# A hybrid decoder layer on one core: table strips shifted on chip, and the order of the odd output projections

## The chip, the cores and the metric

The kernel runs on 1 core of one Trainium2 chip. The metric is device time in microseconds (us) of one execution; several executions are given by their median.

## What is computed

One decoder layer on x (2048 positions x 1024 channels), all in float32, cut to what matters:

```python
hn = rmsnorm(x, norm_g)
a_in, a_gate, c_in, c_b, c_c, c_gate, q, q_gate = split(hn @ w_in)   # 384 x6, 256 x2
# A: 24 groups of 16 channels, each a diagonal complex state space of 64 states
s[l] = lam_bar * s[l-1] + b_bar @ u[l];  y = Re(C s) + D u
g = gelu(y);  y_ssm = g * sigmoid(g @ w_glu + b_glu) * silu(a_gate)
# B: short causal convolution of width 3
y_conv = c_b * conv3(c_c * c_in) * silu(c_gate)
# M: 4-head attention from the positions into 256 fixed memory tokens
y_mem = softmax(q k^T / 8) v * silu(q_gate)
out = rmsnorm(x + concat(y_ssm, y_conv, y_mem) @ w_out, final_norm_g)
```

## The kernel before

**Tiling.** The 2048 positions are four quarters of 512 columns. Every float32 operand of a large matmul is split into a high and a low part (`split`, L86: a cast on ScalarE, L87, and a subtraction on VectorE, L78), and each product is three matmuls (`mm3`, L80, lines 82 to 84). Weights come in tiles of 512 KB through `wtile` (L159): a load on SP into one of two staging buffers, then the split into one of three buffers. An output row tile of a projection is 512 columns of one accumulation bank.

**Stages.** `first` prepares quarter 0; `prep(q)` (L731) loads the input rows of a quarter in four tiles of 128, sums their squares on ScalarE (L112), scales them and transposes them into the quarter's normalised input `hn`, which has one buffer. For each quarter the main line is a chain of projections (`ain`, `agate`, `qproj`, `qgate`, `conv`). `ssm(hf)` (L527) handles two quarters at once in eight tables of three groups: states per chunk of eight positions, a scan on VectorE, then outputs; its results go to DRAM (`g_dram`, L604) and come back in another layout in `glu(q)` (L998, `gr`), which splits them, multiplies by `w_glu`, gates, and splits the three gated state tiles (L1016). That last split overwrites what all nine products of the quarter's gate read. `attention(q, j)` (L917) has nine steps for each of two pairs of heads. `outproj(q)` (L1067) adds the residual and normalises. Quarters 1 and 3 are projected straight from on-chip results; 0 and 2 park theirs in DRAM.

**Tables.** `gen_table(b)` (L427) runs four times, for six groups each. It makes the products M and R, then the short kernel of each group (`ps_k`, L459; `kS`, L460) and its value at distance 0 (`k0r`, L465 and L466), transposes them (L469) and assembles `Kp`, 96 rows of 15 x 16 numbers (L470). `Kp` goes to `k_dram` (L471), and eight transfers (L474), one per position of a chunk, read it back, each shifted by 16 columns, into the table's fourth section, all on GpSimd's queue. One copy (L476) reorders that section, and the table is stored in `t_dram` (L479). Tables use two buffers of the pool `stab`, tag `tb`. `gen_turns` (L482) makes the rotation factors in buffers of the pool `xst`, tag `x`, which the input rows of `prep(1)` use next, and stores them in `t_dram` (L494).

**Order.** Each part is a generator, and the nesting of `interleave`, `weave`, `merge` and `chain` (L820 to L856) fixes the order in which instructions are traced: so many steps of a side line per step of the main line, by a rate. A scheduler then fixes each engine's queue when the program is built: with a clock of its own estimates it takes, for each engine, the earliest traced instruction whose inputs and buffers it holds to be ready. On the chip each queue runs in that order and waits where an estimate was short. The lines that set the order around the change are these (L1189 to L1204):

```python
a0 = att(0)
interleave(chain(kv, ain1), islice(a0, 6), 1.5)
interleave(chain(agate(1), qproj(1), conv(1, 0), qgate(1), conv(1, 1), conv(1, 2)),
           chain(merge(ssm(0), chain(a0, att(1)), 0.6), glu(1)), 3.7)
...
interleave(outproj(1), prep(2), 0.3, 2)
...
interleave(chain(ain(3), main(3)), chain(merge(ssm(1), att(3), 0.3), glu(3)), 3.5, 4)
fetch_y(2)
interleave(outproj(3), glu(2), 1.0)
```

**Output projection.** For each half of the 1024 columns, `outproj` takes the eight 128-row pieces of y in four steps of two: step 0 is state tiles 0 and 1, step 1 state tile 2 and convolution tile 0, step 2 convolution tiles 1 and 2, step 3 attention. Even quarters take them as 0, 1, 3, 2 (`pairs`), odd ones as 3, 2, 1, 0 (`back`, L1021). The residual rows are loaded at its start, on GpSimd's queue (L1060), into the two buffers `big0` and `big1` that attention's probabilities use.

Of the kernel before, what the change touches and what calls it, by code (L numbers as in the profile page):

```python
# [46 lines left out]
def hymba_layer_kernel(  # L47
# [96 lines left out]
    g_dram = dram.tile([NQ, WS, QL], F32, name="g_dram")  # L144
    k_dram = dram.tile([NB, GB * NH, 15 * NH], F32, name="k_dram")
    t_dram = dram.tile([NS, P, GS * TR], F32, name="t_dram")
# [42 lines left out]
    def st_(name, shape=(P, NG)):  # L189
        return sconst.tile(list(shape), F32, name="s_" + name)  # L190
# [8 lines left out]
    Eh, Gm = st_("Eh", (GB * NH, NH)), st_("Gm", (GB * NH, GB))  # L199
    Kp = st_("Kp", (GB * NH, 15 * NH))  # L200
    kS = st_("kS", (P, GB * NH))
    k0S, k0r = st_("k0S", (GB * NH, GB, NH)), st_("k0r", (GB * NH, NH))

    def ssm_prologue():
# [218 lines left out]
        V.tensor_reduce(Eh, idq.rearrange("q g h -> q h g"), AX.X, ALU.add)  # L423
        G.memset(Kp[:, 0:7 * NH], 0.0)


    def gen_table(b):  # L427
# [34 lines left out]
        flat = lambda a: a[:, gs, :].rearrange("p g h -> p (g h)")  # L462
        T.matmul(k0.rearrange("q g h -> q (g h)"), flat(B1), flat(R0), start=True, stop=True)
        tt(k0S, k0, Gm.unsqueeze(2).broadcast_to([GB * NH, GB, NH]), ALU.mult)
        V.tensor_reduce(k0r, k0S.rearrange("q g h -> q h g"), AX.X, ALU.add)  # L465
        V.scalar_tensor_tensor(Kp[:, 7 * NH:8 * NH], Eh, Dc[:, b:b + 1], k0r, ALU.mult, ALU.add)  # L466
        yield
        kb = ps_tr.tile([P, P], F32, tag="tr", name=f"tr_k{b}")[:GB * NH]
        T.transpose(kb, kS, ident)  # L469
        S.copy(Kp[:, 8 * NH:].rearrange("q (t h) -> q h t", h=NH), kb.rearrange("q (h t) -> q h t", h=NH)[:, :, :TCH - 1])  # L470
        nc.gpsimd.dma_start(k_dram[b], Kp)  # L471
        Tq = sec[:, :, 3]
        for j in range(TCH):
            nc.gpsimd.dma_start(Tq[j::TCH], k_dram[b].rearrange("(g h) n -> h g n", h=NH)[:, :, (TCH - 1 - j) * NH:(TCH - 1 - j) * NH + P])  # L474
        yield
# [150 lines left out]
    def first():  # L626
# [6 lines left out]
        wa = [wsl.tile([P, 2, KT, P], F32R, tag="wl", name=f"wai{t}") for t in range(3)]  # L633
        ngt, ones = pro.tile([1, DM], F32, name="ngt"), pro.tile([1, P], F32, name="ones")
        wm = pro.tile([P, QL], mybir.dt.bfloat16, name="wm")
        junk = stab.tile([P, DM], F32, tag="tb", name="junkx")
        ks = ((0, 2), (2, 4), (4, 8))
# [204 lines left out]
    def merge(a, b, rate):  # L842
# [9 lines left out]
        yield from b  # L852

    def chain(*gens):
        for g_ in gens:
            yield from g_  # L856
# [128 lines left out]
    def glu(q):  # L985
# [10 lines left out]
        for t in range(3):  # L996
            gr = swk.tile([P, QL], F32, tag="ain", bufs=2, name=f"gr{q}{t}")
            nc.gpsimd.dma_start(gr, g_dram[q, t * P:(t + 1) * P])  # L998
            split(y_ssm[:, 0, t], y_ssm[:, 1, t], gr)
            yield  # L1000
# [19 lines left out]
    yk = [("ssm", 0), ("ssm", 1), ("ssm", 2), ("conv", 0), ("conv", 1), ("conv", 2), ("mem", 0), ("mem", 1)]  # L1020
    pairs, back = (0, 1, 3, 2), (3, 2, 1, 0)  # L1021

# [26 lines left out]
    def residual(q, last=False):  # L1049

        if last:
            h = [late["att"].tile([P, DM], F32, tag="qh", bufs=2, name=f"h{q}{i}") for i in range(2)]
            for i in range(2):
                load_x(h[i], q, i)
            hb = late["big"].tile([P, 2, DM], F32, tag="big0", name=f"h{q}")
            return h + [hb[:, i] for i in range(2)], hb
        h = [late["big"].tile([P, 2, DM], F32, tag=f"big{z}", name=f"h{q}{z}") for z in range(2)]
        for z in range(2):
            for u in range(2):
                nc.gpsimd.dma_start(h[z][u * NCH:(u + 1) * NCH], xq[q, u][:, 2 * z:2 * z + 2])  # L1060
        return h

    def wout(q, nh, kp, dst=None, st="w"):
        src = w_out[0, kp * 256:(kp + 1) * 256, nh * 512:(nh + 1) * 512]
        return wtile(src, 256, 512, f"wo{q}{nh}{kp}", V, dst, st)

    def outproj(q):  # L1067
        h = residual(q)
        for nh in range(2):
# [4 lines left out]
            for kp in order:  # L1074
                w = wout(q, nh, kp)
                for i in range(4):
                    omm(q, pss[i], i, kp, w, ps_=order)
                    yield
# [107 lines left out]
    def att(q):  # L1186
        return chain(attention(q, 0), attention(q, 1))

    a0 = att(0)  # L1189
    interleave(chain(kv, ain1), islice(a0, 6), 1.5)  # L1190
    interleave(chain(agate(1), qproj(1), conv(1, 0), qgate(1), conv(1, 1), conv(1, 2)),
               chain(merge(ssm(0), chain(a0, att(1)), 0.6), glu(1)), 3.7)

    def main(q):
        return chain(qproj(q), agate(q), qgate(q), conv(q, 0), conv(q, 1), conv(q, 2))

    interleave(outproj(1), prep(2), 0.3, 2)
    interleave(chain(ain(2), main(2)), merge(glu(0), att(2), 0.5), 1.5, 4)
    fetch_y(0)
    interleave(outproj(0), prep(3), 0.3, 2)  # L1200
    interleave(chain(ain(3), main(3)), chain(merge(ssm(1), att(3), 0.3), glu(3)), 3.5, 4)
    fetch_y(2)
# [31 lines left out]
```

## Time and profile before

| what | value |
|---|---|
| runs | 893.05, 894.93, 895.01 us; median 894.93 |
| the profiled execution | 894.48 us, of which its span 892.7 us |
| TensorE (PE) busy | 838.2 us, 94% of the span |
| VectorE (DVE) busy | 612.6 us, 69% |
| ScalarE (ACT) busy | 393.9 us, 44% |
| GpSimd (POOL) busy | 52.4 us, 6% |
| transfers issued by SP and ScalarE | 130.6 MB, 50.1% of 16 engines' span |
| transfers issued by GpSimd | 11.38 MB, 5.2% |
| mean granted TensorE clock | 0.967 |

The span runs from the first to the last instruction of one execution that the hardware profiler took. Busy time is a sum over the whole span; where an engine idles shows only in the views by stretch and by wait. A matmul's shown duration overlaps that of the next, so rates are read from the count in a stretch. A wait names the engine and line that ended it last. The granted clock is TensorE's, as a share of full speed. SP and the queue parts of other engines (SPq, ACTq) count as no busy time.

### The profile page before, as it was taken

How to read it: one execution, taken by the hardware profiler on the slowest of the kernel's cores; microseconds unless marked ns; L12 is line 12 of the kernel's file. 1: busy time of each engine (PE TensorE's matmuls, PEld its weight loads, DVE VectorE, ACT ScalarE, POOL GpSimd, SP SyncE). 2: the span in 40 equal slices, each digit the busy share in tenths (PEclk: the TensorE clock that was granted, in tenths of full speed). 3: DMA queues.
4: the chain of work that ended last, by engine and by line, in shares of the span. 5: the costliest groups of instructions: out<-in, count | busy, mean ns of one | idle time of the engine just before them, and what ended most of it. 6: DMA issues, size and time to landing. Idle time of an engine off the chain costs nothing. (4 is left out here: it accounts for less than half of the span.)

```text
span 892.7 us, 11743 instructions
## 1 busy us (share of the span) xinstructions
PE 838.2 (94%) x4182; PEld 693.4 (78%) x4182; DVE 612.6 (69%) x1287; ACT 393.9 (44%) x767; POOL 52.4 (6%) x93
## 2 busy tenths in 40 slices
PE   8899999929999999939999999999999999899996
PEld 5887788828888888728888888888888888688885
DVE  7479959954779888754446675536568989586563
ACT  5233424435554455633426466333444336454511
POOL 2000102220000000000000010100000000100000
PEclk9999899958999999979999999999999999999999
DMA  8265447795456642283384563565757744566361
GB/s 184 77 176 170 118 132 228 230 256 195 136 164 182 204 136 80 71 188 107 95 272 150 149 165 106 145 173 182 207 144 224 215 146 126 152 166 187 120 188 48
DMA packets 165525, 142.74 MB, mean 160 GB/s; under 512 B 41178, under 2 KB 141594, under 8 KB 165467
## 3 DMA queue, kind: packets, MB, share of 16 engines
q1 hardware_dynamic: 161480, 130.34, 50.0%
q0 software_dynamic: 3904, 11.38, 5.2%
q8 instruction: 33, 0.54, 0.2%
q10 hardware_dynamic: 82, 0.27, 0.1%
q14 instruction: 26, 0.20, 0.1%
HBM read 114.86 MB, written 27.11 MB: 159 GB/s over the span
## 5 line engine op out<-in xcount | busy, mean ns | idle before, releaser
L82 PE MATMUL psai<-hn,wai 128*128 128x256 f32 (+1 forms) x144 | 47.7, 337 | 2.4 <-ACT hn L87 2.3
L83 PE MATMUL psai<-hn,wai 128*128 128x256 f32 (+1 forms) x144 | 47.8, 334 | 1.7 <-DVE hn L78 1.7
L78 DVE TENSOR_TENSOR wo<-wo_st,wo 128x1024 fp32r<-128x1024 f32 x27 | 33.0, 1223 | 23.3 <-ACT wo L87 23.0
L84 PE MATMUL psai<-hn,wai 128*128 128x256 f32 (+1 forms) x144 | 47.3, 331 | 0.0
L87 ACT CAST wo<-wo_st 128x1024 fp32r<-128x1024 f32 x27 | 28.4, 1051 | 39.8 <-PE po L84 19.8
L82 PE MATMUL psag<-hn,wag 128*128 128x512 f32 x96 | 38.4, 400 | 0.0
L82 PE MATMUL pscc<-hn,wcc 128*128 128x512 f32 x96 | 38.4, 400 | 0.0
L82 PE MATMUL psci<-hn,wci 128*128 128x512 f32 x96 | 38.4, 400 | 0.0
L84 PE MATMUL psag<-hn,wag 128*128 128x512 f32 x96 | 37.7, 393 | 0.7 <-DVE wag L78 0.7
L83 PE MATMUL pscc<-hn,wcc 128*128 128x512 f32 x96 | 38.2, 398 | 0.0
L84 PE MATMUL pscb<-hn,wcb 128*128 128x512 f32 x96 | 37.9, 395 | 0.2 <-DVE wcb L78 0.2
L82 PE MATMUL pscb<-hn,wcb 128*128 128x512 f32 x96 | 38.0, 396 | 0.0
L83 PE MATMUL pscg<-hn,wcg 128*128 128x512 f32 x96 | 38.0, 396 | 0.0
L84 PE MATMUL pscg<-hn,wcg 128*128 128x512 f32 x96 | 38.0, 396 | 0.0
L82 PE MATMUL pscg<-hn,wcg 128*128 128x512 f32 x96 | 38.0, 396 | 0.0
L84 PE MATMUL psci<-hn,wci 128*128 128x512 f32 x96 | 38.0, 396 | 0.0
L83 PE MATMUL psci<-hn,wci 128*128 128x512 f32 x96 | 37.9, 395 | 0.0
L83 PE MATMUL pscb<-hn,wcb 128*128 128x512 f32 x96 | 37.7, 393 | 0.0
L84 PE MATMUL pscc<-hn,wcc 128*128 128x512 f32 x96 | 37.7, 393 | 0.0
L937 ACT ACTIVATE pe<-sps,nm 128x256 f32<-128x256 f32 x64 | 29.6, 473 | 18.2 <-DVE nm L935 17.9
L83 PE MATMUL psag<-hn,wag 128*128 128x512 f32 x96 | 37.5, 391 | 0.0
L82 PEld LDWEIGHTS psai<-hn,wai 128*128 128x128 f32 x144 | 29.0, 204 | 5.1 <-ACT hn L87 3.0
(708 smaller groups left out, 2478.2 us busy)
## 6 DMA issues: line engine op xcount, KB each, us to landing
wo_st<-in_w_out_dram SPq DMA_DIRECT2D x32, 512.0 KB, 4.0
tb<-t_dram SPq DMA_DIRECT2D x16, 960.0 KB, 5.1
out_dram<-h SPq DMA_DIRECT2D x32, 256.0 KB, 4.0
wag_st<-in_w_in_dram SPq DMA_DIRECT2D x12, 512.0 KB, 6.4
wci_st<-in_w_in_dram SPq DMA_DIRECT2D x12, 512.0 KB, 3.8
wcc_st<-in_w_in_dram SPq DMA_DIRECT2D x12, 512.0 KB, 3.8
wcb_st<-in_w_in_dram SPq DMA_DIRECT2D x12, 512.0 KB, 4.0
wcg_st<-in_w_in_dram SPq DMA_DIRECT2D x12, 512.0 KB, 3.8
```

The costliest lines, as they stand in the source:

```text
L78: e.tensor_tensor(o, a, b, op)
L82: T.matmul(ps, lh, rh, start=first, stop=False, **kw)
L83: T.matmul(ps, lh, rl, start=False, stop=False, **kw)
L84: T.matmul(ps, ll, rh, start=False, stop=last, **kw)
L87: S.copy(hi, src)
L937: S.activation(pe[:, a, h], sps[h][:, a], AF.Exp, bias=nm_[:, a, h:h + 1], accum_out=sm[:, a, h:h + 1])
```

## The change

Four things. `Kp` becomes 16 rows of six strips, filled by transposing each group's short kernel alone, and the eight shifted transfers read it in place, on SP; `k_dram` goes. The reloads in `glu` and the residual loads go from GpSimd's queue to SP's, and the residual loads are traced after the third weight tile of the projection's first half. Odd projections take the steps as 0, 1, 2, 3. In quarters 1 and 3, `glu` is traced after `ssm` and four empty steps, in one line beside attention, not after both; in quarter 1 what is left of that line follows the main line. The norm row, the ones and the scratch of `first` share one buffer.

```diff
@@ -142,7 +142,6 @@
     bg = const.tile([P, 3], F32, name="bg")
     a_dram = dram.tile([NQ, WS, QL], F32, name="a_dram")
     g_dram = dram.tile([NQ, WS, QL], F32, name="g_dram")
-    k_dram = dram.tile([NB, GB * NH, 15 * NH], F32, name="k_dram")
     t_dram = dram.tile([NS, P, GS * TR], F32, name="t_dram")
     y_dram = dram.tile([2, KT, P, QL], F32, name="y_dram")
@@ -197,7 +196,7 @@
     B1, B2, C1, C2, R0 = (st_(q, (P, NG, NH)) for q in ("B1", "B2", "C1", "C2", "R0"))
     Dc = st_("Dc", (GB * NH, NB))
     Eh, Gm = st_("Eh", (GB * NH, NH)), st_("Gm", (GB * NH, GB))
-    Kp = st_("Kp", (GB * NH, 15 * NH))
+    Kp = st_("Kp", (NH, GB, 15 * NH))
     kS = st_("kS", (P, GB * NH))
     k0S, k0r = st_("k0S", (GB * NH, GB, NH)), st_("k0r", (GB * NH, NH))
@@ -421,7 +420,7 @@
         idq = ident[:GB * NH, :GB * NH].rearrange("q (g h) -> q g h", h=NH)
         V.tensor_reduce(Gm, idq, AX.X, ALU.add)
         V.tensor_reduce(Eh, idq.rearrange("q g h -> q h g"), AX.X, ALU.add)
-        G.memset(Kp[:, 0:7 * NH], 0.0)
+        G.memset(Kp[:, :, 0:7 * NH], 0.0)
 
     def gen_table(b):
@@ -460,18 +459,24 @@
         S.copy(kS, kt.rearrange("k g h -> k (g h)"))
         k0 = ps_tr.tile([P, GB, NH], F32, tag="tr", name=f"ps_d{b}")[:GB * NH]
         flat = lambda a: a[:, gs, :].rearrange("p g h -> p (g h)")
-        T.matmul(k0.rearrange("q g h -> q (g h)"), flat(B1), flat(R0), start=True, stop=True)
+        T.matmul(k0.rearrange("q g h -> q (g h)"), flat(R0), flat(B1), start=True, stop=True)
         tt(k0S, k0, Gm.unsqueeze(2).broadcast_to([GB * NH, GB, NH]), ALU.mult)
         V.tensor_reduce(k0r, k0S.rearrange("q g h -> q h g"), AX.X, ALU.add)
-        V.scalar_tensor_tensor(Kp[:, 7 * NH:8 * NH], Eh, Dc[:, b:b + 1], k0r, ALU.mult, ALU.add)
-        yield
-        kb = ps_tr.tile([P, P], F32, tag="tr", name=f"tr_k{b}")[:GB * NH]
-        T.transpose(kb, kS, ident)
-        S.copy(Kp[:, 8 * NH:].rearrange("q (t h) -> q h t", h=NH), kb.rearrange("q (h t) -> q h t", h=NH)[:, :, :TCH - 1])
-        nc.gpsimd.dma_start(k_dram[b], Kp)
+        V.scalar_tensor_tensor(k0r, Eh, Dc[:, b:b + 1], k0r, ALU.mult, ALU.add)
+        yield
+        for x_ in range(2):
+            kb = ps_tr.tile([P, 3, P], F32, tag="tr", name=f"tr_k{b}{x_}")[:NH]
+            for g in range(3):
+                T.transpose(kb[:, g, :], kS[:, (3 * x_ + g) * NH:(3 * x_ + g + 1) * NH], ident)
+            for g in range(3):
+                S.copy(Kp[:, 3 * x_ + g, 8 * NH:].rearrange("q (t h) -> q h t", h=NH),
+                       kb[:, g].rearrange("q (h t) -> q h t", h=NH)[:, :, :TCH - 1])
+        kd0 = ps_tr.tile([P, GB, NH], F32, tag="tr", name=f"tr_d{b}")[:NH]
+        T.transpose(kd0.rearrange("q g h -> q (g h)"), k0r, ident[:GB * NH, :GB * NH])
+        V.tensor_copy(Kp[:, :, 7 * NH:8 * NH], kd0)
         Tq = sec[:, :, 3]
         for j in range(TCH):
-            nc.gpsimd.dma_start(Tq[j::TCH], k_dram[b].rearrange("(g h) n -> h g n", h=NH)[:, :, (TCH - 1 - j) * NH:(TCH - 1 - j) * NH + P])
+            nc.sync.dma_start(Tq[j::TCH], Kp[:, :, (TCH - 1 - j) * NH:(TCH - 1 - j) * NH + P])
         yield
         S.copy(s["T"].rearrange("p g (h t) -> p g h t", t=TCH), Tq.rearrange("p g (t h) -> p g h t", t=TCH))
         for x_ in range(2):
@@ -631,9 +636,9 @@
         xt += [wst.tile([P, DM], F32, tag="ws", name=f"x0{i}") for i in range(2, 4)]
         wstg = stab.tile([P, KT, WS], F32, tag="tb", name="wai_st")
         wa = [wsl.tile([P, 2, KT, P], F32R, tag="wl", name=f"wai{t}") for t in range(3)]
-        ngt, ones = pro.tile([1, DM], F32, name="ngt"), pro.tile([1, P], F32, name="ones")
+        jx = stab.tile([P, 3 * DM], F32, tag="tb", name="junkx")
+        junk, ngt, ones = jx[:, :DM], jx[0:1, DM:2 * DM], jx[0:1, 2 * DM:2 * DM + P]
         wm = pro.tile([P, QL], mybir.dt.bfloat16, name="wm")
-        junk = stab.tile([P, DM], F32, tag="tb", name="junkx")
         ks = ((0, 2), (2, 4), (4, 8))
         halves = [slice(z * QL, (z + 1) * QL) for z in range(2)]
         nc.sync.dma_start(xt[0][0:NCH], xq[0, 0, :, 0])
@@ -851,6 +856,10 @@
                     yield
         yield from b
+    def pause(n):
+        for _ in range(n):
+            yield
+
     def chain(*gens):
         for g_ in gens:
             yield from g_
@@ -995,7 +1004,7 @@
                 nc.sync.dma_start(us[t], y_dram[q // 2, 5 + t])
         for t in range(3):
             gr = swk.tile([P, QL], F32, tag="ain", bufs=2, name=f"gr{q}{t}")
-            nc.gpsimd.dma_start(gr, g_dram[q, t * P:(t + 1) * P])
+            nc.sync.dma_start(gr, g_dram[q, t * P:(t + 1) * P])
             split(y_ssm[:, 0, t], y_ssm[:, 1, t], gr)
             yield
         for m in range(3):
@@ -1018,7 +1027,7 @@
 
     yk = [("ssm", 0), ("ssm", 1), ("ssm", 2), ("conv", 0), ("conv", 1), ("conv", 2), ("mem", 0), ("mem", 1)]
-    pairs, back = (0, 1, 3, 2), (3, 2, 1, 0)
+    pairs, back = (0, 1, 3, 2), (0, 1, 2, 3)
     def fetch_y(q):
@@ -1057,7 +1066,7 @@
         h = [late["big"].tile([P, 2, DM], F32, tag=f"big{z}", name=f"h{q}{z}") for z in range(2)]
         for z in range(2):
             for u in range(2):
-                nc.gpsimd.dma_start(h[z][u * NCH:(u + 1) * NCH], xq[q, u][:, 2 * z:2 * z + 2])
+                nc.sync.dma_start(h[z][u * NCH:(u + 1) * NCH], xq[q, u][:, 2 * z:2 * z + 2])
         return h
     def wout(q, nh, kp, dst=None, st="w"):
@@ -1065,7 +1074,6 @@
         return wtile(src, 256, 512, f"wo{q}{nh}{kp}", V, dst, st)
     def outproj(q):
-        h = residual(q)
         for nh in range(2):
             ns = slice(nh * 512, (nh + 1) * 512)
             pss = [ps_mm.tile([P, 512], F32, tag="mm", name=f"po{q}{nh}{b}") for b in range(3)]
@@ -1073,6 +1081,8 @@
             order = back if q % 2 else pairs
             for kp in order:
                 w = wout(q, nh, kp)
+                if nh == 0 and kp == order[2]:
+                    h = residual(q)
                 for i in range(4):
                     omm(q, pss[i], i, kp, w, ps_=order)
                     yield
@@ -1188,17 +1198,20 @@
     a0 = att(0)
     interleave(chain(kv, ain1), islice(a0, 6), 1.5)
-    interleave(chain(agate(1), qproj(1), conv(1, 0), qgate(1), conv(1, 1), conv(1, 2)),
-               chain(merge(ssm(0), chain(a0, att(1)), 0.6), glu(1)), 3.7)
+    side = merge(chain(ssm(0), pause(4), glu(1)), chain(a0, att(1)), 0.72)
+    for _ in weave(chain(agate(1), qproj(1), conv(1, 0), qgate(1), conv(1, 1), conv(1, 2)), side, 3.6):
+        pass
     def main(q):
         return chain(qproj(q), agate(q), qgate(q), conv(q, 0), conv(q, 1), conv(q, 2))
+    for _ in side:
+        pass
     interleave(outproj(1), prep(2), 0.3, 2)
     interleave(chain(ain(2), main(2)), merge(glu(0), att(2), 0.5), 1.5, 4)
     fetch_y(0)
     interleave(outproj(0), prep(3), 0.3, 2)
-    interleave(chain(ain(3), main(3)), chain(merge(ssm(1), att(3), 0.3), glu(3)), 3.5, 4)
+    interleave(chain(ain(3), main(3)), merge(chain(ssm(1), pause(4), glu(3)), att(3), 0.42), 3.5, 4)
     fetch_y(2)
     interleave(outproj(3), glu(2), 1.0)
     outproj_last(2)
```

## Rows read from the trace of the kernel before

**Rows 1.** TensorE's waits: engine, tile, line, releaser: us in total, times, longest

```profile
PE trq L176 <- DVE q11a L107: 16.6, 1, 16.6
...
PE po L82 <- ACT ymem L87: 10.6, 1, 10.6
...
PE psg L82 <- ACT yssm L87: 3.5, 1, 3.5
```

**Rows 2.** Busy by stretch: length, PE, PEld, DVE, ACT, POOL, clock, DMA, GB/s

```profile
140.00:182.00 42.00, 39.40 (x241) 34.30 (x239) 41.26 (x88) 17.15 (x26) 9.26 (x18) 1.00 0.82 240
...
180.04:196.88 16.84, 0.28 (x3) 0.10 (x2) 7.72 (x21) 5.81 (x17) 5.17 (x10) 0.57 1.06 277
...
379.53:398.03 18.50, 4.29 (x25) 2.93 (x24) 9.61 (x17) 6.23 (x13) 1.38 (x3) 0.80 0.97 210
...
398.03:401.00 2.97, 2.97 (x7) 2.39 (x8) 2.87 (x7) 0.43 (x1) 0.34 (x1) 0.51 0.35 103
...
401.00:406.00 5.00, 5.00 (x23) 4.10 (x23) 2.49 (x8) 2.39 (x5) 0.55 (x1) 1.00 0.00 0
```

**Rows 3.** Timeline of SP in stall A: start, us, engine, line, operation

```profile
177.48 0.60 SPq L494 DMA_DIRECT2D t_dram<-ge  x1
...
185.49 1.11 SPq L620 DMA_DIRECT2D xq<-in_x_dram  x2
```

**Rows 4.** Timeline of GpSimd, SP, VectorE and ScalarE in stall B

```profile
378.07 1.22 POOL L1060 DMA_DIRECT2D h<-in_x_dram  x2 [21.56 <-ACT um L963]
...
382.65 1.13 SPq L620 DMA_DIRECT2D xq<-in_x_dram  x2
...
383.39 0.69 DVE L78 TENSOR_TENSOR yssm<-ua,yssm 128x512 fp32r<-128x512 f32 x1
...
386.64 0.68 DVE L1013 SCALAR_TENSOR_TENSOR ua<-gt,ua 128x512 f32<-128x512 f32 x1
...
395.61 0.63 ACT L112 ACTIVATE junkq<-xq 128x512 f32<-128x512 f32 x1 [9.59 <-DMA xq<-in_x_dram]
...
396.24 0.60 ACT L87 CAST yssm<-ua 128x512 fp32r<-128x512 f32 x1
```

**Rows 5.** Timeline of SP and GpSimd ahead of stall C

```profile
767.35 0.90 SPq L604 DMA_DIRECT2D g_dram<-ge  x2
...
776.33 0.58 POOL L998 DMA_DIRECT2D gr<-g_dram  x1 [8.14 <-DMA g_dram<-ge]
```

**Rows 6.** Timeline of all engines, the second table, 133 to 156 us

```profile
133.63 0.27 PE L469 MATMUL tr_k<-ident,s_kS 128*96 128x128 f32 x1
...
133.74 0.60 PE L176 MATMUL trm<-ident,m 128*128 128x128 f32 x4
...
136.78 0.35 ACT L470 COPY s_Kp<-tr_k 96x112 f32<-96x112 f32 x1
...
137.42 0.57 POOL L471 DMA_DIRECT2D k_dram<-s_Kp  x1 [23.96 <-ACT s_Kp L470]
...
140.57 4.10 POOL L474 DMA_DIRECT2D gt<-k_dram  x8 [2.58 <-DMA k_dram<-s_Kp]
...
148.35 1.21 SPq L479 DMA_DIRECT2D t_dram<-gt  x2
...
153.97 1.81 DVE L78 TENSOR_TENSOR gt<-s_L,s_B 128x768 f32<-128x768 f32 x2
```

**Rows 7.** Timeline of SP and TensorE, quarter 3's last weights

```profile
760.34 0.37 SPq L163 DMA_DIRECT2D wcg_st<-in_w_in_dram  x1
...
782.71 0.63 PE L82 MATMUL pscg<-hn,wcg 128*128 128x512 f32 x1
```

**Rows 8.** Timeline of TensorE and VectorE, start of quarter 3's output projection

```profile
790.50 0.39 PE L82 MATMUL po<-wo,ymem 128*128 128x512 f32 x1
...
799.56 0.70 DVE L78 TENSOR_TENSOR yssm<-ua,yssm 128x512 fp32r<-128x512 f32 x1
```

**Rows 9.** Groups of ScalarE, 779 to 802 us: busy, mean ns, idle before

```profile
L87 ACT CAST yssm<-gr 128x512 fp32r<-128x512 f32 x4 | 2.5, 621 | 9.1 <-DMA gr<-g_dram 9.1
```

## The prediction

> **What bounds the kernel now.** I read the page's engine line first (in the table above: TensorE busy 94% of the span), then TensorE's waits, then busy time by stretch around each wait, then the queues of the other engines there. TensorE's busy time cannot shrink, since no matmul goes away; only its idle time can. Three waits hold most of it [rows 1]: 16.6 us before the transposes of quarter 1's input rows (stall A), 10.6 us before a matmul of the first output projection (stall B), 3.5 us before a gate matmul of quarter 3 (stall C). By stretch [rows 2]: in A 16.84 us pass with 0.28 busy; in B 18.50 with 4.29 busy, so 14.2 idle; and after B the granted clock is 0.51 (the lower level, 1.2 GHz): 7 matmuls in 2.97 us, where the next stretch, at 1.00, does 23 in 5.00 (0.217 each). Those 7 lost 1.5 us, so B costs 15.7.
>
> What ends the stalls is not what their names say. **A** ends when input rows arrive: their load goes out at 185.49, after a table store issued at 177.48 has landed and freed its buffer [rows 3]. The DMA engines are full then (share 1.06 in the A row) [rows 2]. **B** ends late on ScalarE's queue: at 395.61 it starts a row sum of quarter 2 for which it had waited 9.59 us on an input load (issued 382.65), while the split of state tile 2, computed by 387.32, stands behind it until 396.24 [rows 4]. The attention tile, which this projection takes first, stands behind both. At 378.07 the residual loads went out beside that input load [rows 4]. **C** ends on a reload of state rows that GpSimd issues 776.33 after waiting 8.14 us for stores issued from 767.35 [rows 5].
>
> **The change, part by part.**
>
> *Table rows from on-chip memory.* Per table the path loses the store to DRAM and the wait for it (137.42 to 140.57, 3.15 us) [rows 6]; eight issues on GpSimd (4.10) become eight on SP at 0.45 (two in 0.90 [rows 5]), 3.6 us. It gains five more strip copies on ScalarE; no row shows a 16-partition strip, so between nothing and the 0.35 of today's 96-partition copy each, and I take 0.35, since the columns are the same: 1.75 us [rows 6]. Net 3.15 + 0.5 - 1.75 = -1.9 us per table. No transfer between two on-chip tiles is in the trace; last gather issue to store is 3.7 us now, copy included (144.67 to 148.35), so the landing could cost up to that much more or less, and I take it as unchanged, the destination and piece count being the same.
>
> TensorE does seven transposes per table instead of one. Four take 0.60, so 6 x 0.15 x 4 tables = 3.6 us [rows 6]. They fall into 120 to 182, ahead of A's wait, which absorbs them: cost 0 while A stands, 3.6 if A closes.
>
> Does a shorter table path shorten A? The fourth table began at 153.97, after the second's store of 148.35 [rows 6], so 1.9 us pass on. But VectorE is busy 41.26 of the 42 us before A [rows 2], so an earlier table finds no free VectorE time. I take -2; bounds -7.6 (four tables in sequence) and +3.6 (eight SP issues put ahead of the input loads).
>
> *GpSimd's transfers to SP.* 32 gathers, 12 reloads of state rows and 12 residual loads: 56 issues x 0.45 = 25 us on SP, spread over the span, hidden by SP's free time. What counts is what they wait for. On GpSimd nothing but tiny powers stood behind a wait; on SP the weight loads do. The last weights of quarter 3 left at 760.34 for a matmul at 782.71, 22 us ahead [rows 7], so one 8 us wait is covered: cost 0, up to 2 us where three such waits (24 us) follow one another. The Trainium skill (DMA: Bandwidth & Descriptors, section "Anatomy of one DMA") speaks against this edit: DMA engines wait for nothing, any semaphore wait is spent on the issuing sequencer ahead of dispatch. The trace agrees (GpSimd's 8.14 us); it is the mechanism of the third rival, and by the rule alone the sum would be that rival's time.
>
> *State space first in quarter 1.* The first step needs state tiles 0 and 1; the later of their splits ran at 383.39 and ended 384.1, 4.6 us into B. A step is 24 matmuls x 0.217 = 5.2 us, to 389.3. Tile 2 is computed at 387.32; its split (0.6 on ScalarE, 0.7 on VectorE) is done by 388.6, if ScalarE takes it ahead of the row sum [rows 4]. Then convolution, 5.2 us more per step, while the attention tile waits out the row sum without cost. What is late next is state tile 1: 4.6 of the 15.7 us stay. So -11. If ScalarE's order stays, tile 2 comes at 396.24 + 1.3 = 397.5: 4.6 + 8.2 idle, and 1.5 of low clock, leaves 14.3, or -1.4. Bounds -15.7 and -1.4. I take the first because gates traced among the attention steps, not after them, come earlier in both queues.
>
> *State space first in quarter 3.* Today this projection starts at 790.50 on attention data that is ready, and the split of a state tile still starts at 799.56 [rows 8]. Put first, it would be waited for: 800.3 - 790.5 = 9.8, and 1.5 of low clock, 11.3 us. The tiles are late because ScalarE waits 9.1 us there for reloads of the next quarter's state rows [rows 9]; that can be cured by the gates' earlier place and four empty steps that cover the reload's round trip. Bounds 0 and +11.3. I take +4, nearer to 0: the last reload arrives as now, three gates need 27 matmuls (6 us), and main matmuls last about as long.
>
> *Stall C.* The empty steps and the residual loads traced later (after the third weight tile) should let the reload land sooner. -2 of 3.5; bounds -3.5 and +3 (the reload now queues behind weights).
>
> The moved norm row and ones vector, the larger memset and the swapped operands cost nothing: they run in the first 10 us or are of equal size.
>
> **Sum.** -2 (A) - 11 (B) - 2 (C) + 4 (quarter 3) = -11 us. The profiled execution took 894.48 (span 892.7 and 1.8 around it), 0.45 below the median of the runs, so both serve as the base: 883.5.
>
> **Rivals.**
> 1. *The late state tiles are exposed twice* (slower). ScalarE keeps its row sum ahead of tile 2 in quarter 1 (-1.4) and its reload waits ahead of the gates in quarter 3 (+11.3): with A's -2, +7.9, or 902. It decides once state tiles land over 4 us after the main matmuls end in quarter 3. For it: the splits at 396.24 and 799.56. Against: both queues are rewritten by the new trace order. Chance 0.17.
> 2. *Gain and loss cancel.* B gives 11, quarter 3 takes 11.3, the rest nothing: 894.5. The likeliest way for nothing to show. Chance 0.13.
> 3. *SP's queue holds the weights.* Three waits in a row exceed the 22 us lead at up to four places, +2 each: 891.5. For it, GpSimd's long waits; against, weights issued that early. Chance 0.07.
> 4. *All stalls close.* A -7.6, B -15.7, C -3.5, quarter 3 0, the transposes uncovered +3.6: -23.2, or 871. Needs everything at its best bound. Chance 0.14.
>
> **How the numbers follow.** The forecast has 0.49. About 0.3% (2.7 us) is what a measurement of this kernel can tell from no change. Faster: forecast 0.49, rival 4 0.14, 0.02 of rival 3 and 0.01 of rival 2: 0.66. Same: 0.12 of rival 2 and 0.02 of rival 3: 0.14. Slower: rival 1 0.17 and 0.03 of rival 3: 0.20. The range goes from rival 4 (870) to rival 1 (902); what is left out is everything going right with a better order of ScalarE's queue, or a new stall at both odd projections. The forecast's own range is 876 to 891.
>
> **What would show it.** B: no wait over 5 us at the start of the first output projection, which reads state tiles first and attention last, and no granted clock of about 0.5 after it. Quarter 3: under 5 us idle ahead of its first state matmul; more says rival 1 or 2. C: under 2 us before the gate matmul. A: still over 12 us, ended by input rows, and the second table's last transpose to its store 2 us shorter than today's 15. GpSimd issues no DMA; SP's wait list names state rows or strips. I am wrong if B stays within 3 us of 15.7, if quarter 3 opens a wait of 8 us or more, or if A moves by over 8.

## The result and the profile after

The changed kernel takes 881.25 us (median of 4 executions, 878.84 to 881.69) where the kernel before takes 894.97 beside it: a ratio of 0.9852, 95% interval 0.9825 to 0.988, so 13.7 us faster. Measured once more on another occasion it was 0.9865 (0.9841 to 0.989). The forecast was 883.5.

To see where the time went I cut both traces at four marks of TensorE's timeline: the first matmul of quarter 0's queries and the first input matmul of quarters 1, 2 and 3. In the changed kernel they are these rows (start, us, engine, line, operation):

```profile
80.69 0.39 PE L82 MATMUL psq<-hn,wq 128*128 128x512 f32 x1
...
204.34 0.58 PE L82 MATMUL psai<-hn,wai 128*128 128x256 f32 x1
...
431.01 0.39 PE L82 MATMUL psai<-hn,wai 128*128 128x512 f32 x1
...
617.80 0.39 PE L82 MATMUL psai<-hn,wai 128*128 128x512 f32 x1
```

The same marks before stand at 82.30, 203.01, 442.54 and 629.01, and the last output matmul ends at 884.60 (after: 871.51). That cuts the span into stretches, in us, read from one profiled execution of each kernel; a second one of the changed kernel gives the same stretches within 0.6:

| stretch | before | after | difference | forecast |
|---|---|---|---|---|
| start, to the first mark | 82.3 | 80.7 | -1.6 | 0 |
| tables and stall A, to quarter 1 | 120.7 | 123.7 | +2.9 | -2 |
| quarter 1 and stall B, to quarter 2 | 239.5 | 226.7 | -12.9 | -11 |
| to quarter 3 | 186.5 | 186.8 | +0.3 | 0 |
| quarter 3, stall C, both last projections | 255.6 | 253.7 | -1.9 | -2 + 4 |
| after the last matmul | 8.1 | 8.0 | -0.1 | 0 |

**TensorE's waits after** (engine, tile, line, releaser: us in total, times, longest), against [rows 1]; lines are numbered by the changed kernel, mostly up to 9 off the old ones:

```profile
PE trq L175 <- DVE xb L751: 13.2, 1, 13.2
PE trq L175 <- DVE xq L751: 6.1, 1, 6.1
PE po L82 <- ACT yssm L87: 5.2, 4, 2.2
```

Stall A is still there, cut in two (6.1 and 13.2 in place of 16.6). Stalls B and C are gone from the list; in their place stand four short waits for splits of state tiles. By stretch (as [rows 2]: length, PE, PEld, DVE, ACT, POOL, clock, DMA, GB/s):

```profile
181.27:187.38 6.11, 0.01 (x2) 0.04 (x1) 3.77 (x10) 3.33 (x13) 0.55 (x1) 0.72 1.04 345
189.32:202.55 13.23, 0.00 (x1) 0.00 (x1) 4.65 (x11) 7.24 (x15) 1.10 (x2) 0.50 0.86 195
...
379.19:392.00 12.81, 9.95 (x46) 7.48 (x47) 12.38 (x19) 7.14 (x12) 0.00 (x0) 1.00 0.98 225
392.00:400.00 8.00, 8.00 (x37) 6.52 (x36) 0.00 (x0) 1.75 (x5) 0.00 (x0) 1.00 0.90 201
```

In A TensorE does nothing and its clock falls to 0.50. At the first projection (379.19) it is busy 9.95 of 12.81 us and then all the time, the clock at 1.00: no stretch at the low clock follows, where before there was one [rows 2].

**Stall B after**, on the timelines of ScalarE and SP, against [rows 4]:

```profile
383.05 1.25 SPq L1069 DMA_DIRECT2D h<-in_x_dram  x2
384.36 4.83 SPq L625 DMA_DIRECT2D xq<-in_x_dram  x4
...
384.14 0.62 ACT L87 CAST yssm<-ua 128x512 fp32r<-128x512 f32 x1
...
387.47 0.62 ACT L87 CAST ymem<-uq 128x512 fp32r<-128x512 f32 x1 [2.22 <-DVE uq L990]
...
389.97 0.61 ACT L87 CAST yssm<-ua 128x512 fp32r<-128x512 f32 x1
396.67 0.63 ACT L112 ACTIVATE junkq<-xq 128x512 f32<-128x512 f32 x1 [6.09 <-DMA xq<-in_x_dram]
```

The input rows come no sooner: the row sum starts at 396.67, a microsecond later than before, again after a wait. But the split of state tile 2 (389.97) and that of the attention tile (387.47) now stand ahead of it in ScalarE's queue, not behind.

**The second table after**, by engine, against [rows 6]:

```profile
133.47 0.82 PE L470 MATMUL tr_k<-ident,s_kS 128*16 128x128 f32 x6
...
135.29 1.35 ACT L472 COPY s_Kp<-tr_k 16x112 f32<-16x112 f32 x6
...
139.73 0.25 PE L475 MATMUL tr_d<-ident,s_k0r 96*16 96x96 f32 x1
...
140.93 0.24 DVE L476 COPY s_Kp<-tr_d 16x96 f32<-16x96 f32 x1
...
141.23 5.35 SPq L479 DMA_DIRECT2D gt<-s_Kp  x8
...
149.96 1.24 SPq L484 DMA_DIRECT2D t_dram<-gt  x2
```

From the short kernels' transposes to the store pass 16.5 us, where it was 14.7. Six strip copies take 1.35, but the value at distance 0 now goes over TensorE and back over VectorE, and its transpose comes 6.3 us after the others.

**The third table** moves further, and with it the rows that stall A waits for. Before:

```profile
149.04 0.27 PE L469 MATMUL tr_k<-ident,s_kS 128*96 128x128 f32 x1
...
168.41 1.19 SPq L479 DMA_DIRECT2D t_dram<-gt  x2
...
174.35 1.17 SPq L620 DMA_DIRECT2D xb<-in_x_dram  x2
```

After:

```profile
156.16 0.82 PE L470 MATMUL tr_k<-ident,s_kS 128*16 128x128 f32 x6
...
165.12 0.25 PE L475 MATMUL tr_d<-ident,s_k0r 96*16 96x96 f32 x1
...
175.90 1.19 SPq L625 DMA_DIRECT2D xq<-in_x_dram  x2
...
179.59 1.27 SPq L484 DMA_DIRECT2D t_dram<-gt  x2
```

Its transpose of the value at distance 0 comes 9.0 us after the others, and its store goes out 11.2 us later than before. The second and fourth input rows (`xb`) use a table buffer; their loads start at 192.22 and not at 174.35 (at 187.35 in e6 below, where no gather stands ahead of them). The first row (`xq`) is loaded sooner than before, at 175.90 and not at 185.49 [rows 3]. So the longer of the two waits in A is now for the second row, where before the wait was for the first.

**Quarter 3's projection after**, on ScalarE and TensorE, against [rows 8] and [rows 9]:

```profile
773.84 0.62 ACT L87 CAST yssm<-gr 128x512 fp32r<-128x512 f32 x1 [6.30 <-DMA gr<-g_dram]
774.37 0.61 ACT L87 CAST yssm<-ua 128x512 fp32r<-128x512 f32 x1
...
775.03 0.50 PE L82 MATMUL po<-wo,yssm 128*128 128x512 f32 x1 [2.25 <-ACT yssm L87]
```

ScalarE still waits for a reload of the next quarter's state rows, and the split that the projection needs stands behind it. It costs 2.25 us here and 0.95 at a split a few matmuls later. The idle time of the whole stretch is the same, 3.50 us before and 3.46 after; what it gains is clock. After stall C the kernel before ran at 0.60, the changed one keeps 1.00 after its short waits (before, then after, columns as in [rows 2]):

```profile
780.00:784.00 4.00, 4.00 (x11) 3.14 (x12) 3.78 (x5) 2.62 (x3) 0.58 (x1) 0.60 1.04 218
```

```profile
775.10:779.00 3.90, 2.95 (x12) 2.11 (x13) 3.87 (x8) 2.40 (x5) 0.00 (x0) 1.00 0.70 181
```

At the 0.217 us of a matmul at full clock, 11 of them would have taken 2.4 us in place of 4.0, so C had cost some 5.1 us and not 3.5.

### The profile page after: what moved, and what is told of

Its sections match the earlier page's. It is cut to its first block, busy times and chain, and to the rows that moved or that the text cites. A ratio compares the mean times of both kernels' runs of the same rounds, so it can differ in the third digit from the quotient of the medians.

```text
span 879.5 us, 11746 instructions
## 1 busy us (share of the span) xinstructions
PE 834.2 (95%) x4206; PEld 689.0 (78%) x4206; DVE 613.5 (70%) x1291; ACT 398.0 (45%) x787; POOL 20.5 (2%) x33
## 5 line engine op out<-in xcount | busy, mean ns | idle before, releaser
L83 PE MATMUL psai<-hn,wai 128*128 128x256 f32 (+1 forms) x144 | 47.1, 327 | 1.7 <-DVE hn L78 1.7
L82 PE MATMUL psai<-hn,wai 128*128 128x256 f32 (+1 forms) x144 | 47.1, 330 | 0.0
L84 PE MATMUL psai<-hn,wai 128*128 128x256 f32 (+1 forms) x144 | 46.8, 325 | 0.0
L82 PE MATMUL po<-wo,yssm 128*128 128x512 f32 x84 | 33.2, 401 | 5.2 <-ACT yssm L87 5.2
```

Source lines behind the costliest of these rows:

```text
L82: T.matmul(ps, lh, rh, start=first, stop=False, **kw)
L83: T.matmul(ps, lh, rl, start=False, stop=False, **kw)
L84: T.matmul(ps, ll, rh, start=False, stop=last, **kw)
```

## Experiments

Each kernel was compared with the kernel before on the same chip. "Quarter 1" is the stretch from quarter 1's mark to quarter 2's, "quarter 3" the one from quarter 3's mark to the last matmul; "place" says what stood first in ScalarE's queue, the last split of a state tile or the first sum of quarter 2's third and fourth input rows. The stretches come from one profiled execution of each kernel; that of e3 took 4.2 us more than its median, the others lie within 3 us of theirs.

| run | us | ratio, 95% interval | A | quarter 1 | quarter 3 | place |
|---|---|---|---|---|---|---|
| before | 894.97 | 1 | 120.7 | 239.5 | 255.6 | sum |
| changed | 881.25 | 0.9852 (0.9825 to 0.988) | 123.7 | 226.7 | 253.7 | split |
| e1_old_order | 893.15 | 0.998 (0.996 to 1.0) | 123.3 | 231.3 | 262.8 | split |
| e2_order_only | 889.4 | 0.994 (0.9916 to 0.9964) | 123.2 | 234.2 | 258.8 | split |
| e3_old_nesting | 886.12 | 0.9919 (0.9894 to 0.9944) | 124.6 | 227.9 | 259.1 | split |
| e4_old_reloads | 892.51 | 0.9985 (0.9966 to 1.0005) | 122.4 | 237.3 | 253.5 | sum |
| e7_residual_gpsimd | 892.44 | 0.9974 (0.9958 to 0.999) | 123.9 | 235.5 | 255.5 | sum |
| e8_residual_sp_early | 881.06 | 0.9846 (0.9814 to 0.9878) | 123.8 | 225.8 | 251.9 | split |
| e15_before_splits_first | 887.77 | 0.9923 (0.99 to 0.9947) | 121.4 | 233.8 | 255.8 | split |
| e5_old_tables | 878.58 | 0.9819 (0.9786 to 0.9853) | 121.3 | 226.8 | 253.5 | split |
| e6_gathers_gpsimd | 879.7 | 0.983 (0.9805 to 0.9855) | 122.6 | 227.2 | 252.5 | split |
| e10_three_rows | 876.94 | 0.9802 (0.9778 to 0.9825) | 120.8 | 224.6 | 252.9 | split |
| e14_rows_first | 874.09 | 0.9767 (0.9742 to 0.9791) | 116.3 | 226.8 | 253.7 | split |

### The order and the nesting, one at a time

The changed kernel with the old order of the odd projections:

```diff
-    pairs, back = (0, 1, 3, 2), (0, 1, 2, 3)
+    pairs, back = (0, 1, 3, 2), (3, 2, 1, 0)
```

> The changed kernel (881.25 us), only the odd projections take attention first and state space last again. Theory (the order is needed): in the changed kernel quarter 1's first projection starts at 379.2 and the last attention tile's split runs at 387.5; put first, it is waited for some 9 us, with about 1.5 us of low clock after it and 2.6 us of today's gaps gone: about +8, so 889. Rival a (the earlier gates alone do it): the splits are on time whichever comes first, at most 2 us of wait: 880 to 883. Rival b (the gain has nothing to do with stall B): 881, with a first projection that starts no later.

893.15 us: almost the whole gain is lost, more than I had said. Quarter 1 loses 4.6 of it and quarter 3 loses 9.1, where I had expected nothing: with the gates traced early and the attention tile taken first, quarter 3's projection is interrupted by a gate matmul of quarter 2 that waits 4.1 us for its weights (engine, tile, line, releaser, as above). With shorter waits, two of them at attention's tiles (1.6 and 1.7), the idle time of the stretch is 8.7 us, where the changed kernel has 3.5; the rest of the loss is matmul time (254.0 in place of 250.2), with a clock of 0.75 from 784 to 790.

```profile
PE psg L82 <- ACT wg L87: 4.5, 2, 4.1
PE po L82 <- ACT ymem L87: 2.9, 2, 1.7
```

The kernel before with the new order alone (the same line, the other way round):

> The kernel before (894.97 us) with nothing but the new order of the odd projections; the gates still come after the attention steps. Theory (the order needs the earlier gates): quarter 1 starts on state tiles split at 383.4 and then waits until about 397.5 for tile 2 behind the row sum, -1.4 at most; quarter 3 waits for state splits, up to +11.3: 897 to 905. Rival a (the order alone does it): stall B falls by 11, quarter 3 opens no wait: about 884. Rival b (the loss in quarter 3 cancels the gain in quarter 1): 894 to 896.

889.4 us, between the two rivals. My claim that tile 2 would come behind the row sum fell: in this build the split runs at 388.4, ahead of it. Quarter 1 gains 5.3 and not more, because the row sum now runs at 400.87 with the weight splits of the second half behind it; VectorE gets to the additions that free TensorE's accumulators only after them:

```profile
PE po L82 <- DVE h L78: 4.9, 1, 4.9
```

Quarter 3 loses 3.2, as the order puts tiles first that are late there.

The changed kernel with the old nesting (gates behind the attention steps):

```diff
-    side = merge(chain(ssm(0), pause(4), glu(1)), chain(a0, att(1)), 0.72)
-    for _ in weave(chain(agate(1), ...), side, 3.6):
-        pass
+    interleave(chain(agate(1), ...), chain(merge(ssm(0), chain(a0, att(1)), 0.6), glu(1)), 3.7)
...
-    interleave(chain(ain(3), main(3)), merge(chain(ssm(1), pause(4), glu(3)), att(3), 0.42), 3.5, 4)
+    interleave(chain(ain(3), main(3)), chain(merge(ssm(1), att(3), 0.3), glu(3)), 3.5, 4)
```

> The changed kernel with the state-space steps and attention steps nested as before (gates behind the attention steps), state space still first in the odd projections. Theory: the splits of state tiles 1 and 2 fall behind the row sum in quarter 1 (wait of 8 to 15 us at the first projection) and the first state matmul of quarter 3 waits up to 11 us: 890 to 903. Rival a (the order alone does it): within 2 us of 881. Rival b (what counts is the reloads on SP): within 2 us of 881 too, but with GpSimd's reloads put back it would be slow (next run).

886.12 us, under the theory's range. Quarter 1 is only 1.2 longer than in the changed kernel and has its splits ahead of the row sum: the earlier gates are not what cures stall B. Quarter 3 is 5.4 longer: that is where they count (stall C's wait is there, at 5.1 us). In quarter 3 the order with the old nesting loses (258.8 in e2, against 255.6), the nesting with the old order loses (262.8 in e1, which has the other edits too), and together they gain (253.7).

### What decides stall B

The changed kernel with its reloads on GpSimd again, the residual rows at the projection's start:

```diff
     def outproj(q):
+        h = residual(q)
...
-                if nh == 0 and kp == order[2]:
-                    h = residual(q)
...
-                nc.sync.dma_start(h[z][u * NCH:(u + 1) * NCH], xq[q, u][:, 2 * z:2 * z + 2])
+                nc.gpsimd.dma_start(h[z][u * NCH:(u + 1) * NCH], xq[q, u][:, 2 * z:2 * z + 2])
...
-            nc.sync.dma_start(gr, g_dram[q, t * P:(t + 1) * P])
+            nc.gpsimd.dma_start(gr, g_dram[q, t * P:(t + 1) * P])
```

> The changed kernel with the reloads of state rows and the residual rows issued by GpSimd again, the residual rows traced at the start of the projection. Theory (who issues them costs nothing): within 2 us of 881.25. Rival a (the later residual rows let quarter 2's input rows land sooner, and that is the gain at stall B): the wait for the row sum reaches the projection again, +3 to +8. Rival b (SP's waits for state rows hold weights back in the changed kernel): -1 to -4, so 877 to 880.

892.51 us. This edit I had costed at nothing, and undoing it takes back 10.6 us in quarter 1. In this build a row sum stands ahead of tile 2's split again. Two runs then split it: the residual rows alone back on GpSimd (all of the diff above but its last two lines), and the residual rows early but on SP (its first three changed lines alone).

> The changed kernel, only the residual rows back on GpSimd at the start of the projection; state rows stay on SP. In the built queue ScalarE has one row sum of quarter 2's input rows ahead of the split of state tile 2 again. Theory (that place in ScalarE's queue is what decides stall B): a wait of 8 to 12 us inside the first projection, ended by that split, with low clock after it; 889 to 893, as with both reloads put back. Rival a (it was the state rows' reload on SP): within 2 us of 881. Rival b (what counts is how many bytes the DMA engines carry ahead of the input rows): as in the theory, and the next run the same.

> The changed kernel, the residual rows still on SP but traced at the start of the projection as before. In the built queue ScalarE has all three splits ahead of the row sums. Theory (that place decides, not the time at which the residual rows are fetched): no wait over 3 us inside the first projection, 880 to 883. Rival (residual rows fetched early take the DMA engines from the input rows): 886 to 893.

892.44 and 881.06 us: the theory's numbers in both. With the residual rows on GpSimd, ScalarE's timeline reads

```profile
387.50 0.62 ACT L87 CAST ymem<-uq 128x512 fp32r<-128x512 f32 x1 [2.21 <-DVE uq L990]
395.85 0.63 ACT L112 ACTIVATE junkq<-xq 128x512 f32<-128x512 f32 x1 [7.73 <-DMA xq<-in_x_dram]
...
397.89 0.62 ACT L87 CAST yssm<-ua 128x512 fp32r<-128x512 f32 x1
```

and TensorE waits 9.5 us for that last split, which in the changed kernel runs at 389.97. The row sum's data is there at about the same time (395.85 and 396.67); only its place differs. These two runs differ in nothing but the queue of the residual loads, and the loads go out at nearly the same moments: 378.86 and 383.36 on GpSimd, 377.07 and 381.89 on SP (378.23 and 383.05 in the changed kernel, so tracing them later moved nothing here). So neither the time of the residual fetch nor the bytes it moves count; the queue does, through the order that was built from it. That the residual loads, standing ahead of the input rows on SP's queue, make the builder's estimate of the rows' arrival later, and so put the sum behind the split, is how I read it: the order of the built queue was seen, the estimate was not.

Last, the place by itself: the kernel before, with a constraint on ScalarE's queue and nothing else.

```diff
             split(y_ssm[:, 0, m, :], y_ssm[:, 1, m, :], us[m])
+            if q == 1:
+                ahead.append(nc.cur_bb.bb.instructions[-2].name)
...
         put(q, "mem", j, u_)
+        if q == 1:
+            ahead.append(nc.cur_bb.bb.instructions[-2].name)
...
             for z in range(2):
                 sumsq(xt[:, z * QL:(z + 1) * QL], ss[:, z:z + 1], junk)
+            if q == 2 and i > 1:
+                for ins in list(nc.cur_bb.bb.instructions[n_:]):
+                    if ins.engine == mybir.EngineType.Activation:
+                        for name in ahead:
+                            tc.add_manual_dep(ins, name, ..., reason="splits_first")
```

> The kernel before, with one change to ScalarE's queue and none to what is computed, loaded or in which order projections take their tiles: the sums of quarter 2's third and fourth input rows are put behind the splits of quarter 1's state tiles and attention tile. Theory (the place of those sums in ScalarE's queue is the cause of stall B, whichever tile is taken first): the wait of 10.6 us before the attention tile's split falls under 3, the stretch from the first projection of quarter 1 to that of quarter 2 (239.5 us) comes down by 5 to 9, and the time to 886 to 890. Rival a (state space first is the cure): the wait moves to the next late tile and the time stays within 2 us of 894.7. Rival b (the rows themselves bound the stage): the same, with the wait at the transposes of quarter 2's rows.

887.77 us, 0.9923: attention is still taken first, nothing is computed or loaded otherwise, and half of the change's gain is there (5.7 us of it in quarter 1). The wait of 10.6 us is gone:

```profile
386.98 0.62 ACT L87 CAST yssm<-ua 128x512 fp32r<-128x512 f32 x1 [1.30 <-DVE ua L1024]
387.58 0.62 ACT L87 CAST ymem<-uq 128x512 fp32r<-128x512 f32 x1
395.75 0.63 ACT L112 ACTIVATE junkq<-xq 128x512 f32<-128x512 f32 x1 [7.56 <-DMA xq<-in_x_dram]
```

The input rows come as before (395.75 and 395.61), so it is the place alone. The other 7.1 us that the change gains in quarter 1 are not split up further: from 376 us to quarter 2's mark the changed kernel idles 3.2 us at a mean clock of 1.00, this one 5.9 at 0.94. Over all builds quarter 1 takes 235.5 to 239.5 with a sum in front, 231.3 to 234.2 with the splits in front, and 224.6 to 227.9 where state space is taken first as well and the residual rows are on SP.

### The tables

The tables as before, the rest as changed (the strips through `k_dram` and the gathers on GpSimd):

> The changed kernel with the tables made as before (strips through DRAM, eight gathers on GpSimd, the norm row and ones in buffers of their own); order, gates and reloads as changed. Theory (the table edit brings nothing, its eight gathers on SP's queue hold quarter 1's input rows back a little): quarter 1's first projection starts at about 203 and the wait there is one of 16 us, as before; -1 to -3 against 881.25, so 878 to 880. Rival (the on-chip strips are part of the gain): quarter 1 starts 3 us or more after 204.3: 884 or more.

878.58 us. Against 0.9852 the interval (0.9786 to 0.9853) does not settle it; the stretch of the tables points to a loss: 121.3 here, 121.4 in e15, 120.7 before, against 122.4 to 124.6 with the new tables on SP; e2, which has the old ones, is the exception at 123.2. So the table edit shows no gain, and by the stretches it costs about 2 us.

The gathers on GpSimd, from the on-chip strips:

```diff
-            nc.sync.dma_start(Tq[j::TCH], Kp[:, :, ...])
+            nc.gpsimd.dma_start(Tq[j::TCH], Kp[:, :, ...])
```

> The changed kernel, strips still shifted from the on-chip tile, but the gathers issued by GpSimd. Theory (in the changed kernel the last table's eight gathers, 6.3 us of issues from 185.8, stand on SP's queue ahead of the loads of quarter 1's input rows, which go out at 192.2): those loads go out 4 to 6 us sooner and quarter 1 starts at 198 to 200: 875 to 878. Rival (the rows wait for their buffer or for the DMA engines, not for SP): within 1.5 us of 881.

879.7 us; the theory fell. In the changed kernel the gathers do stand ahead of the input rows on SP:

```profile
179.59 1.27 SPq L484 DMA_DIRECT2D t_dram<-gt  x2
...
185.80 6.32 SPq L479 DMA_DIRECT2D gt<-s_Kp  x8
192.22 1.19 SPq L625 DMA_DIRECT2D xb<-in_x_dram  x2
```

and with them on GpSimd the rows are ordered at 187.35, 4.9 us sooner. But they land only 1.2 us sooner; the row sum on ScalarE waits for them until 196.07 in place of 197.27:

```profile
187.35 3.58 SPq L625 DMA_DIRECT2D xb<-in_x_dram  x4
...
196.07 0.63 ACT L112 ACTIVATE junkq<-xb 128x512 f32<-128x512 f32 x1 [5.51 <-DMA xb<-in_x_dram]
```

### A version that beats both

Three input rows in the free table buffer, on the tables as before:

```diff
-        return [t[:, i * DM:(i + 1) * DM] for i in range(2)]
+        return [t[:, i * DM:(i + 1) * DM] for i in range(3)]
...
-            xt = xb[i // 2] if xb and i % 2 else xst.tile(...)
+            xt = xb[i] if xb and i < 3 else xst.tile(...)
```

> A candidate: order, gates and reloads as changed, tables as before, and quarter 1's first three input rows (not the second and fourth) loaded into the free table buffer, which holds three; only the fourth waits for a buffer of the rotation factors. In the run with the tables as before the two rows in that buffer were loaded at 174 to 176, and the first row, which the projection needs first, at 185.1. Theory (stall A is that wait for a buffer): the first half's rows are there by about 183, quarter 1 starts at 190 to 194 instead of 202.6, and the fourth row costs a shorter wait in the second half: 868 to 874. Rival (the DMA engines are full there, so that rows ordered sooner land no sooner, or weights land later): quarter 1 starts at 200 or later, 876 to 880.

876.94 us, faster than the changed kernel, but by no more than the rival allowed; from e5 (878.58), which has the same tables and two such rows, it is not clear of noise. The rows were there early, and TensorE still began at 202.5. VectorE and ScalarE read

```profile
178.84 0.63 ACT L112 ACTIVATE junkq<-xb 128x512 f32<-128x512 f32 x1
...
189.61 1.04 ACT L87 CAST wai<-wai_st 128x1024 fp32r<-128x1024 f32 x1 [3.04 <-DMA wai_st<-in_w_in_dram]
...
190.69 1.22 DVE L78 TENSOR_TENSOR wai<-wai_st,wai 128x1024 fp32r<-128x1024 f32 x1 [3.26 <-ACT wai L87]
192.72 1.28 DVE L746 SCALAR_TENSOR_TENSOR xb<-xb,q10o,ng_b 128x1024 f32<-128x1024 f32 x1 [0.35 <-DVE q10o L108]
```

The second half of the first row was summed from 178.84, but the row's scaling (192.72) stood behind a weight split that waited for a load. It is stall B's pattern on another engine. The same kind of constraint as in e15, here on the weight splits (behind the first two rows' scaling) and on the fourth row's sum (behind the second row's split), gave the next version:

> The last candidate (0.980 of the kernel before) with the order of two queues set by hand in quarter 1: VectorE scales the first and second input rows ahead of the second and third weight splits, and ScalarE splits their transposes ahead of the fourth row's sum. There the rows had landed and were summed by 182.4, but VectorE took the scaling only at 192.7 and 197.8, behind weights that came in late. Theory (stall A is, like B, an order in which work with its data there stands behind work without): quarter 1 starts at 193 to 197 instead of 202.5, and 5 to 8 us are gained: 869 to 872. Rival (the weights, held by full DMA engines, set the start anyway): within 2 us of 877.

874.09 us, 0.9767 (0.9742 to 0.9791): the fastest, 2 us short of the theory, and with an interval that still overlaps that of e10. The scaling runs at 188.55 and quarter 1 starts at 197.19; of the 4.5 us that the stretch before it gains on e10, quarter 1 gives back 2.2. What is left of stall A are 10.9 and 3.5 us; the DMA engines are full there (share 1.08 from 180 to 190, 1.09 in e10).

The changed kernel beside the first of these two runs:

> The changed kernel itself, for a comparison on the same chip: 0.982 to 0.988 of the kernel before.

882.19 us, 0.9865 (0.9841 to 0.989).

## Why the prediction was right, and where it was not

**The total** came out 2 us below the forecast and inside its own range. The place of the gain was right: stall B, to which I gave -11, gave -12.9. That the total is so near is in part luck, since misses cancel: A came out 4.9 us worse than forecast, and B (1.9), the start (1.6) and quarter 3 with C (3.9) better. The prediction also held TensorE's busy time fixed; it fell from 838.2 to 834.2 us, as the mean granted clock rose from 0.967 to 0.975.

**Stall B, reason.** That the late tile waits behind a row sum on ScalarE, and not for its own data, was right (e15). The step that failed is "I take the first because gates traced among the attention steps, not after them, come earlier in both queues": with the old nesting the splits come ahead as well (e2, e3), and with the new one they came behind (e4, e7). With the earlier gates, what keeps the splits ahead is the move of the residual loads to SP, 12 of the 56 issues costed at nothing because SP has time; the order of the projection alone does it with the old nesting (e2). So the split came ahead in the changed kernel, as forecast, but not for the reason that I gave. I asked what those transfers wait for and who waits behind them on SP, but not what their move does to the order in which the other queues are built. What I let stay (4.6 us for state tile 1) was 0.92 and 1.66 us, for tiles 1 and 2.

**Stall A.** -2 was wrong: +2.9. Two terms of the table's path failed. The value at distance 0 had no row of mine, and its transpose came 6.3 us after the others in the second table and 9.0 in the third, where the DRAM round trip saved was 3.15. SP's issues took 0.67 to 0.79 us each (8 in 5.35 to 6.32), not 0.45, which was the price of another transfer. The six strip copies, on the other hand, took 0.23 each, and the landing I took as unchanged was so: 2.6 us in the median, 2.7 before. The path itself was not the one that A hung on: before, the late row waited for a store of rotation factors (L494 in [rows 3]), not of a table, and the change made the rows in a table buffer the late ones. The bound of +3.6 was set by the right mechanism in place, gathers ahead of the input rows, but e6 shows that it costs about 1 us: ordered sooner, the rows of the table buffer took 9.0 us to land in the median, in place of 5.8.

**Quarter 3 and stall C.** +4 and -2 came out as -1.9 together. The 3.5 us of C are gone, and with them the low clock after it, some 1.6 us that I had not counted; the opening costs 2.25 and 0.95. The bound of +11.3 was not reached by any run; the largest loss was e1's, by a wait that I did not have.

**SP and the weights.** As a wait it was costed at nothing, and so it was. SP waited 9.5 us in five pieces for the stores of state rows, at most 3.9 at once:

```profile
SPq L1007 <- DMA g_dram<-ge: 9.5, 5, 3.9
```

TensorE's list of waits has no wait for weights over 0.7 us, and the time of the third rival did not come. That the wait is spent on the issuing queue is what the Trainium skill says (DMA: Bandwidth & Descriptors, "Anatomy of one DMA"); SP's list agrees.

**Rivals.** The first (slower) needed row sum and reload waits to stay in front in both quarters; e4 and e7 are its first half, and they end at 892.5, not 902. The second needed quarter 3 to lose 11.3, and its stretch came out 1.9 shorter. The fourth needed stall A to close, and even e14 closes only part of it.

**Start.** The 1.6 us that the start gained are no part of the change's mechanism: the clock that TensorE was granted differs there from run to run with the same startup code. Between 30 and 40 us (columns as above) the changed kernel has

```profile
30.00:40.00 10.00, 10.00 (x78) 9.12 (x76) 1.73 (x10) 2.15 (x4) 0.00 (x0) 1.00 0.24 77
```

and e4, whose edits lie hundreds of microseconds later,

```profile
30.00:40.00 10.00, 10.00 (x77) 9.83 (x75) 0.39 (x3) 0.84 (x2) 0.00 (x0) 0.88 0.18 52
```

with its first mark at 82.0 (before: 82.3, and 0.88 there too). e2 and e15, with the startup code of the kernel before, reach the mark at 79.9 and 80.9. What sets the clock there was not tried.

## What to carry to other kernels

When a stage stalls, look on each queue for work with its data at hand that stands behind work without, and put the two in order by hand: in quarter 1 that was worth 5.7 us of the stretch, 7 us of the whole (e15), with no other change. For a gap, the Trainium skill says to find what blocks and to make it start sooner or finish faster (Perfetto Trace Analysis, "Optimization Strategy"). The split did start sooner here, but by its place in the queue and not by its data; the input rows that it stood behind came a microsecond later in the changed kernel than before. A transfer moved to another queue can reorder engines that it never touches, so after any such edit read the order of the queues around the old stalls before costing it at nothing. In quarter 3 order and nesting were worth something only as a pair, so undo the parts of a change one at a time before keeping some.

## What was not expected of the hardware

A gather of 48 KB from 16 partitions of an on-chip tile landed no sooner than the same gather from DRAM: 2.6 us in the median, issued by SP, and 2.7 from DRAM, issued by GpSimd. Issued by GpSimd as well (e6), the gather from the tile took 4.0. Eight issues took 5.35 to 6.32 us on SP (0.67 to 0.79 each) and 4.10 to 4.27 on GpSimd (0.51 to 0.53 each, from the tile in e6). The issue of input rows on SP is no fixed price either: two loads took 1.13 us in [rows 4], four took 4.83 in the changed kernel. A full set of DMA engines does not explain it, as their share was 1.08 during the first and 1.07 during the second; the cause stays open.
